# Renewing the normalized input ahead of the token-major values in a two-layer encoder trunk

## The chip, the cores and the metric

The kernel runs on one core of a Trainium2 chip. The metric is the time of one execution on the device in microseconds (us). Three runs of the kernel before took 1825.64, 1826.25 and 1828.06 us; the median is 1826.25 us.

The core has several engines that work side by side, each through its own list of instructions in order: TensorE (PE: matrix products into eight PSUM banks; PEld is its weight load), VectorE (DVE: elementwise work), ScalarE (ACT: functions and copies), GpSimd (POOL: here some small elementwise work, and it issues DMAs) and SyncE (SP: it issues the weight loads). They wait for each other by semaphores.

## The reference

Two layers, each with D_MODEL 1024 and 512 tokens:

```python
h = rmsnorm(x, mix_norm[i])
z = h @ w_in[i]
u_rnn, u_gelu, c_q, ckv_rope, fq, fk, fv, f_logit, gate_logit = split_columns(z)
y_a = rglru_branch(u_rnn, u_gelu, ...) @ w_br_a[i]
y_b = mla_branch(c_q, ckv_rope, ...) @ w_br_b[i]
y_c = fox_branch(fq, fk, fv, f_logit, fox_bf[i]) @ w_br_c[i]
g = sigmoid(gate_logit + gate_b[i]).reshape(B, S, 3, D)
merged = g[:, :, 0] * y_a + g[:, :, 1] * y_b + g[:, :, 2] * y_c
x = x + merged @ w_o[i]
# then a SwiGLU feed-forward and a gated per-layer embedding, each added to x
```

`rglru_branch` is a recurrent branch (convolution, gates, a scan over time), `fox_branch` and `mla_branch` are attentions with 8 heads. What matters here is that `h`, the normalized input, is multiplied with many column blocks of `w_in`: the recurrent inputs, the queries, keys and values of the first attention (called fox), the low-rank inputs of the second, and 3 x 8 blocks of merge gates. Normalizing multiplies each channel of x by a gain and each token by one number r, so r can also be applied after a product, to its result.

## The kernel before, in words

**Layout.** Activations lie feature-major: a page has 128 features on the partitions and 512 tokens in the columns. For accuracy every operand is split into a high part (rounded to float32r) and a low remainder, and each product takes three passes: high by high, high by low, low by high (`mm3`, L239). A split costs a copy on ScalarE and a subtraction on VectorE (`split`, L232). A `pr` page holds both parts of 512 columns, and there are 31 of them (L176); a `pf` page holds 512 float32 columns, and there are 20. Both are handed out from lists, first freed, first taken, and so are the 8 PSUM banks.

**Weights.** `Stream` (L85) loads all weights in the order of use, 256 KB at a time, from SyncE's queue, and splits them (L112 on ScalarE, L113 on VectorE) into a ring of eight units of four 128 by 128 tiles. `dense` (L246) multiplies one column block: for each of its weight tiles (8 for the input's products) three products of 512 columns, into one bank, which an eviction function then reads.

**Order.** The program is traced in a `TileContext` with `schedule_with_timeline_sim=True` (L1386): the order of the instructions on each engine is fixed when the kernel is built, from the order of the program and an estimate of when each could start; weight splits get a higher priority (L111). On the chip each engine then keeps this order.

**A layer's mixers** (`mix`, L441). The input comes as eight pages X, which hold x times the gain and not yet times r; r is known later. First come the recurrent branch's inputs, shared keys, the forget gates and the recurrent gates, all with X and with r applied by the evictions (`scaled`, L278). `lru_tail` (L666) is the recurrent branch's elementwise end: for each of four blocks a combination of two operands, a product, a scan (L677), a product and a split into the pages `yA`. Then follow the keys and queries of heads 0 and 1 (`fox_proj(0, X, st["r"])`, L685 to L687), and the token-major values of all heads (`values`, L608 and L688): 96 products of 512 columns with X as the stationary operand, into four banks; the evictions (L628 on ScalarE, L629 on VectorE) apply r with one number per partition.

**Attention** (L751) goes over 8 heads x 4 blocks of 128 queries. For each block it issues the scores, the softmax on VectorE and ScalarE, transposes and, once per head, the product with the values. Between these it takes pieces of other products off a plan, which has a list for each quarter of the 32 blocks: `fp(p, w)` is the key (w=0) or query (w=1) projection of heads 2p and 2p+1 (8 weight tiles), `mg(0, j, yA)` a merge gate from the input (`gate`, L714, 8 tiles) and the recurrent branch's output product (`branch`, L725, 4 tiles). `fill` (L759) takes about the same number of tiles after each block: seven in the first quarter.

**Renewal.** `renorm` (L691) makes normalized pages Xn: it loads a block of x again from memory by a POOL DMA (L695), scales it by gain and r on VectorE (L696, in the trace at the helper's L218), and splits it (in the trace at L233 on ScalarE and L221 on VectorE). Products of Xn need no r afterwards. Before the change the renewal is part of the first quarter's list beside attention, in three pieces: behind `fp(1, 0)`, `mg(0, 0)` and `mg(0, 1)`, which still take X and r. `drop_x` then frees X and r. From `fp(1, 1)` on all products take Xn.

Of the kernel before, what the change touches and what calls it, by code (L numbers as in the profile page):

```python
# [18 lines left out]
KD = D // 128  # L19
# [147 lines left out]
class Trunk:  # L167
# [273 lines left out]
    def mix(self, layer):  # L441
        nc = self.nc
        L, st, X = layer, self.st, self.xp
# [42 lines left out]
        rT = self.cols(NT)  # L486
# [115 lines left out]
        def fox_proj(p, X, r):  # L602
            return [
                self.dense(self.win(L, C_FK + 128 * p), X, ev_heads(kp, p, r, True, False)),
                self.dense(self.win(L, C_FQ + 128 * p), X, ev_heads(qp, p, r, True, True)),
            ]

        def values(spec, X, rT):  # L608

            V = []  # L610
            bs = [self.banks.take() for _ in range(NT)]
            for k, x in enumerate(X):
                wh, wl = self.w.wide(spec + (k,))
                for j in range(NT):
                    c = slice(j * 128, (j + 1) * 128)
                    self.mm3(bs[j][:, :], x.h[:, c], x.l[:, c], wh, wl, k == 0, k == len(X) - 1)
                    yield
            for j in range(NT):
                g = pr.take()
                V.append(g)  # L620
                dst = g.ap.rearrange("p (h t d) -> p h t d", h=HEADS, t=2)
                src = bs[j].rearrange("p (h d) -> p h d", h=HEADS)
                hi = dst[:, :, 0, :]
                if rT is None:
                    self.split(hi, dst[:, :, 1, :], src)
                else:
                    r = rT[:, j:j + 1]
                    self.act(hi, src, AF.Copy, scale=r)  # L628
                    self.stt(dst[:, :, 1, :], src, r, hi.bitcast(F32), ALU.mult, ALU.subtract)  # L629
                self.banks.give(bs[j])  # L630
            self.V = V


        yA = [None] * 4
# [50 lines left out]
        k0, q0 = fox_proj(0, X, st["r"])  # L685
        self.run(k0)
        self.run(q0)  # L687
        self.run(values(("fv", L), X, rT))  # L688
        Xn = [None] * KD

        def renorm(*ks):  # L691

            for k in ks:
                t, p = pf.take(), pr.take()
                nc.gpsimd.dma_start(t.ap, x_dram[k])  # L695
                self.stt(t.ap, t.ap, self.v(L, V_MIX + k), st["r"].ap, ALU.mult, ALU.mult)  # L696
                self.split(p.h, p.l, t.ap)
                t.free()
                Xn[k] = p
            return  # L700
            yield

        def drop_x():
            for p in X:
                p.free()
            st.pop("r").free()
            return
            yield


        merged = [None] * KD
        out_pages = [None] * KD
# [32 lines left out]
        def merge(n, j, ys, X=Xn, r=None):  # L745
            box = []
            yield from gate(n, j, box, X, r)
            yield from branch(n, j, ys, box)
# [154 lines left out]
        def fp(p, w, X=Xn, r=None):  # L903
            return (fox_proj(p, X, r)[w], 8)

        def mg(n, j, ys, X=Xn, r=None):
            return (merge(n, j, ys, X, r), 12)
# [56 lines left out]
        def done_c():  # L964
            for p in oC:
# [5 lines left out]
        lkv = [(latent(ckv, skv, C_CKV, j), 8) for j in range(2)]  # L971
        tail = chain(gate(2, 2, boxes[2, 2]), gate(2, 3, boxes[2, 3]))
        attention(True, oC, [
            [fp(1, 0, X, st["r"]), (renorm(0, 1), 0), mg(0, 0, yA, X, st["r"]), (renorm(2, 3, 4), 0),
             mg(0, 1, yA, X, st["r"]), (renorm(5, 6, 7), 0), (drop_x(), 0), fp(1, 1), mg(0, 2, yA)],
            [fp(2, 0), mg(0, 3, yA), mg(0, 4, yA), fp(2, 1), mg(0, 5, yA)],
            [fp(3, 0), mg(0, 6, yA), fp(3, 1)] + lq,
            lkv + [mg(0, 7, yA), (free_yA(), 0), (latent_sums(), 0), gt(2, 0), (latent_norm(), 0),
# [413 lines left out]
```

## Time and profile before

| | |
|---|---|
| median of three runs | 1826.25 us (1825.64 to 1828.06) |
| the profiled execution: its own time | 1826.21 us |
| its span, first to last instruction | 1824.4 us |
| mean granted TensorE clock | 0.994 |
| layer 0: values products begin, end | 82.2 us, 104.0 us |
| layer 1: values products begin, end | 975.8 us, 997.6 us |
| weight splits over the span | 590 in the ring and 16 kept, 0.62 us on ScalarE and 0.69 us on VectorE each |

How to read the lines that are shown below: a line of the timeline has the start and the length in us, the engine, the line of the kernel (often a helper's: L237 is `mm`, L218 a combination of a tensor, a number and a tensor, L221 a plain two-operand operation, L225 a scaling, L230 a ScalarE function, L233 the copy of a split), the operation, the tile written and the tiles read, and the shapes; in brackets the idle time ahead of it with what ended it. A group has the same names, then the count, the busy time in us and the mean length in ns, then the idle time before. A line of the waits has who waited for whom, the sum in us, the count and the longest. Matmuls are pipelined, and a matmul's length holds the pipeline's depth: the pace is the distance from start to start. Names: `pf` and `pr` are the pages, `bank` PSUM, `hl` the split weights, `raw` the loaded ones, `vec` the gains, `small` numbers per token.

### The profile page before, as it was taken

The numbers are of one execution on the slowest core, as the hardware profiler recorded it, in microseconds if no ns is written. First come the engines' busy times: TensorE is split into PE (matmuls) and PEld (weight loads), VectorE is DVE, ScalarE is ACT, GpSimd is POOL, SyncE is SP. The second block draws the span as 40 slices with busy tenths as digits, with TensorE's granted clock in tenths as the row PEclk, the third lists the DMA queues.
The fourth block names the chain that finished last, engine by engine and source line by source line (L and its number), as shares of the span: only waits on it lengthen the run. The fifth ranks groups of instructions, "written<-read, shape, count | busy, mean of one in ns | idle before, by whom it ended". The sixth has DMA issues, their size and how long they took to land. (4 is left out here: it accounts for less than half of the span.)

```text
span 1824.4 us, 24163 instructions
## 1 busy us (share of the span) xinstructions
PE 1803.9 (99%) x8476; PEld 1504.5 (82%) x8476; DVE 1209.1 (66%) x2421; ACT 817.5 (45%) x1562; POOL 116.8 (6%) x234
## 2 busy tenths in 40 slices
PE   9899999999999999999999999999999999999998
PEld 7688888888888888888888788888888888888887
DVE  8896678866665555444778966888576555553457
ACT  5766556553333333223448655565523333332233
POOL 1230001100000000000103200010000000000000
PEclk9899999999999999999999999999999999999999
DMA  6142224324322233322433322342232323232331
GB/s 206 59 150 83 81 78 116 100 70 139 95 96 95 96 99 98 109 95 98 133 111 123 105 81 82 90 117 85 87 128 92 99 98 97 95 110 99 98 99 47
DMA packets 98826, 184.17 MB, mean 101 GB/s; under 512 B 13552, under 2 KB 14752, under 8 KB 98704
## 3 DMA queue, kind: packets, MB, share of 16 engines
q1 hardware_dynamic: 89280, 162.04, 27.3%
q0 software_dynamic: 8416, 19.45, 3.9%
q8 instruction: 66, 1.08, 0.2%
q10 hardware_dynamic: 1008, 1.14, 0.2%
q14 instruction: 56, 0.46, 0.1%
HBM read 173.98 MB, written 4.21 MB: 98 GB/s over the span
## 5 line engine op out<-in xcount | busy, mean ns | idle before, releaser
L237 PE MATMUL bank<-pr,hl 128*128 128x512 f32 (+1 forms) x6812 | 1602.3, 392 | 7.0 <-ACT pr L233 6.9
L237 PEld LDWEIGHTS bank<-pr,hl 128*128 128x128 f32 (+1 forms) x6812 | 1270.0, 188 | 268.9 <-ACT pr L233 8.6
L112 ACT CAST hl<-raw 128x512 fp32r<-128x512 f32 x590 | 363.8, 618 | 649.4 <-PE bank L237 438.8
L113 DVE TENSOR_TENSOR hl<-raw,hl 128x512 fp32r<-128x512 f32 x590 | 404.4, 686 | 367.9 <-ACT hl L112 352.0
L221 DVE TENSOR_TENSOR pf<-pf 128x512 f32<-128x512 f32 (+3 forms) x235 | 151.2, 651 | 31.9 <-ACT pf L230 29.8
L221 DVE TENSOR_TENSOR pf<-bank,pf 128x512 f32<-128x512 f32 (+3 forms) x198 | 132.9, 676 | 56.9 <-PE bank L237 31.9
L230 ACT ACTIVATE pf<-pf 128x512 f32<-128x512 f32 (+1 forms) x145 | 86.0, 600 | 112.3 <-DVE pf L221 110.0
L237 PE MATMUL bank<-pr 128*128 128x256 f32 (+5 forms) x704 | 119.5, 301 | 3.5 <-ACT pf L230 3.3
L237 PEld LDWEIGHTS bank<-pr 128*128 128x128 f32 (+1 forms) x704 | 103.4, 190 | 13.7 <-ACT pf L230 3.4
L221 DVE TENSOR_TENSOR pr<-pf,pr 128x512 fp32r<-128x512 f32 (+3 forms) x126 | 85.5, 683 | 4.0 <-ACT pr L233 3.1
L230 ACT ACTIVATE pf<-bank,small 128x384 f32<-128x384 f32 (+3 forms) x130 | 68.9, 531 | 42.0 <-DVE small L838 38.6
L233 ACT CAST pr<-pf 128x512 fp32r<-128x512 f32 (+2 forms) x114 | 70.3, 620 | 29.2 <-DVE pf L218 18.1
L855 ACT CAST pth<-bank 128x128 fp32r<-128x128 f32 (+3 forms) x128 | 54.0, 426 | 65.4 <-PE bank L830 62.3
L838 DVE TENSOR_REDUCE small<-bank 128x1 f32<-128x384 f32 (+3 forms) x128 | 61.7, 484 | 19.2 <-PE bank L237 18.2
L221 DVE TENSOR_TENSOR ptl<-bank,pth 128x128 fp32r<-128x128 f32 (+3 forms) x128 | 61.7, 484 | 12.8 <-ACT pth L855 10.3
L237 PE MATMUL bank<-hl,pr 128*128 128x512 f32 x240 | 55.9, 390 | 0.0
L830 PE MATMUL bank<-identr,pf 128*128 128x128 f32 x320 | 55.7, 273 | 0.0
L237 PEld LDWEIGHTS bank<-hl,pr 128*128 128x128 f32 x240 | 44.9, 188 | 9.2
L225 DVE TENSOR_SCALAR pf<-pf,small 128x384 f32<-128x384 f32 (+3 forms) x128 | 48.4, 383 | 2.6
L230 ACT ACTIVATE pf<-bank,vec 128x512 f32<-128x512 f32 x60 | 41.0, 688 | 16.7 <-PE bank L237 16.2
L218 DVE SCALAR_TENSOR_TENSOR pf<-pf,bank 128x512 f32<-128x512 f32 x48 | 32.6, 683 | 20.8 <-PE bank L237 20.5
L830 PEld LDWEIGHTS bank<-identr,pf 128*128 128x128 f32 x320 | 40.0, 141 | 7.6
(112 smaller groups left out, 792.9 us busy)
## 6 DMA issues: line engine op xcount, KB each, us to landing
raw<-wst SPq DMA_DIRECT2D x606, 256.0 KB, 2.6
pf<-xT POOLq DMA_DIRECT2D x16, 256.0 KB, 3.1
pr<-pr POOLq DMA_DIRECT2D x32, 128.0 KB, 2.7
pf<-xs POOLq DMA_DIRECT2D x16, 256.0 KB, 3.1
pf<-trig POOLq DMA_DIRECT2D x12, 256.0 KB, 3.1
pf<-xT SPq DMA_DIRECT2D x8, 256.0 KB, 5.4
xs<-pf POOLq DMA_DIRECT2D x8, 256.0 KB, 2.7
pf<-pT POOLq DMA_DIRECT2D x4, 256.0 KB, 3.1
```

Of the source, the lines that this page charges most:

```text
L112: self.nc.scalar.copy(hi, src)
L113: self.nc.vector.tensor_tensor(lo, src, hi.bitcast(F32), op=ALU.subtract)
L218: self.nc.vector.scalar_tensor_tensor(out, a, s, b, op0=op0, op1=op1)
L221: self.nc.vector.tensor_tensor(out, a, b, op=op)
L225: self.nc.vector.tensor_scalar(out, a, s1, None, op0=op0)
L230: return self.nc.scalar.activation(out, a, f, **kw)
L233: self.nc.scalar.copy(hi, src)
L237: self.nc.tensor.matmul(out, a, b, start=start, stop=stop, skip_group_check=True)
L830: nc.tensor.transpose(T[:, c], p2.ap[:, c], self.ident[:, :])
L838: nc.vector.reduce_max(R[t][:, 0:1], S[:, :m], axis=AX.X, negate=True)
L855: self.nc.scalar.copy(hi, src)
```

## The change

```diff
         k0, q0 = fox_proj(0, X, st["r"])
         self.run(k0)
         self.run(q0)
-        self.run(values(("fv", L), X, rT))
         Xn = [None] * KD
 
         def renorm(*ks):
...
                 self.split(p.h, p.l, t.ap)
                 t.free()
                 Xn[k] = p
-            return
-            yield
 
         def drop_x():
             for p in X:
                 p.free()
             st.pop("r").free()
-            return
-            yield
-
+
+        renorm(*range(KD))
+        self.run(values(("fv", L), X, rT))
+        drop_x()
...
         attention(True, oC, [
-            [fp(1, 0, X, st["r"]), (renorm(0, 1), 0), mg(0, 0, yA, X, st["r"]), (renorm(2, 3, 4), 0),
-             mg(0, 1, yA, X, st["r"]), (renorm(5, 6, 7), 0), (drop_x(), 0), fp(1, 1), mg(0, 2, yA)],
+            [fp(1, 0), mg(0, 0, yA), mg(0, 1, yA), fp(1, 1), mg(0, 2, yA)],
```

All eight pages are renewed in one call that stands between the keys and queries of heads 0 and 1 and the values, in both layers. The values still take X, and X and r are freed behind them. The key projection of heads 2 and 3 and the first two merge gates take Xn where they took X; their evictions no longer multiply by r, and read the bank directly. Weights, their order and the products are the same.

## The prediction

> **What bounds the kernel now.** I read the page first, then who keeps TensorE waiting, then a table by stage, then the two places of the change row by row, on TensorE and on VectorE.
>
> ```profile
> span 1824.4 us, 24163 instructions
> ...
> PE 1803.9 (99%) x8476; PEld 1504.5 (82%) x8476; DVE 1209.1 (66%) x2421; ACT 817.5 (45%) x1562; POOL 116.8 (6%) x234
> ```
>
> TensorE is busy for 99% of the span; VectorE, with 66%, has room on the average. Who keeps TensorE waiting:
>
> ```profile
> PE bank L237 <- ACT pr L233: 6.9, 3, 3.8
> PE bank L237 <- ACT pf L230: 3.3, 1, 3.3
> ```
>
> The 6.9 us lie in layer 0's start, ahead of anything the change touches. The 3.3 us are a single wait, and it lies in the change's stretch of layer 1. So little can be won, and what can be lost is any time in which a product waits for the renewed input. Whether it will wait is a question to VectorE at that place, not to its average. The table by stage (length, then busy time of PE, PEld, DVE, ACT, POOL, then the granted clock): the first and third rows are the values products of layers 0 and 1, the second a long undisturbed stretch.
>
> ```profile
> 92.00:104.00 12.00, 12.00 (x55) 9.94 (x54) 11.94 (x18) 7.12 (x12) 3.83 (x8) 1.00 0.62 200
> ...
> 300.00:960.00 660.00, 660.00 (x3007) 547.66 (x3006) 407.90 (x743) 250.96 (x462) 24.20 (x45) 1.00 0.32 102
> ...
> 982.00:997.60 15.60, 15.60 (x71) 12.92 (x69) 15.51 (x23) 8.42 (x15) 5.36 (x10) 1.00 0.37 118
> ```
>
> Elsewhere VectorE is busy for 408 of 660 us. Beside the values it is busy for 11.94 of 12.00 us and 15.51 of 15.60 us: it has a queue of its own there, mostly the recurrent branch's tail, which stands ahead of the renewal in the program. This is the row that decides: the change moves a need forward in time, on to an engine that has no free time to serve it sooner.
>
> **The change part by part.** Moved: eight loads, eight scalings (L696), eight copies on ScalarE and eight subtractions on VectorE (both from `split`), per layer. Before, the first projection beside attention and two gates read the raw X, so renewed pages were wanted only 32 weight tiles behind the values. After it, the first product that follows the values wants page 0, and one more page with each three products. TensorE at that place in layer 0, and then in layer 1:
>
> ```profile
> 103.97 0.33 PE L237 MATMUL bank<-pr 128*128 128x128 f32 x2
> 104.14 5.03 PE L237 MATMUL bank<-pr,hl 128*128 128x512 f32 x21
> 109.00 0.40 PE L237 MATMUL bank<-pr 128*128 128x256 f32 x2
> 109.23 4.95 PE L237 MATMUL bank<-pr,hl 128*128 128x512 f32 x21
> ```
>
> ```profile
> 997.66 2.96 PE L237 MATMUL bank<-pr,hl 128*128 128x512 f32 x12
> ...
> 1002.90 1.32 PE L237 MATMUL bank<-pr,hl 128*128 128x512 f32 x5
> ```
>
> From 104.14 to 109.00 us are 21 products: 0.231 us each, 0.69 us for the three of a page. The projection `fp(1, 0)` has 24; its last three run from 109.23 and end at 109.9 us. In layer 1 they run from 1002.90 and end at 1003.6 us.
>
> When are the pages ready? VectorE in layer 0 (four scalings, with a subtraction, a weight split and the first eviction of the values among them):
>
> ```profile
> 103.50 0.74 DVE L218 SCALAR_TENSOR_TENSOR pf<-pf,vec 128x512 f32<-128x512 f32 x1
> 104.17 0.68 DVE L221 TENSOR_TENSOR pr<-pf,pr 128x512 fp32r<-128x512 f32 x1
> 104.77 0.74 DVE L218 SCALAR_TENSOR_TENSOR pf<-pf,vec 128x512 f32<-128x512 f32 x1
> 105.44 0.68 DVE L113 TENSOR_TENSOR hl<-raw,hl 128x512 fp32r<-128x512 f32 x1
> 106.04 0.68 DVE L221 TENSOR_TENSOR pr<-pf,pr 128x512 fp32r<-128x512 f32 x1
> ...
> 109.17 0.74 DVE L218 SCALAR_TENSOR_TENSOR pf<-pf,vec 128x512 f32<-128x512 f32 x1
> 109.83 0.74 DVE L218 SCALAR_TENSOR_TENSOR pr<-bank,small,pr 128x512 fp32r<-128x512 f32 x1
> ```
>
> From start to start a scaling takes 0.67 us and a subtraction or a weight split 0.60 us, so a page costs 1.27 us against the 0.69 us in which TensorE uses it up. What VectorE has from 103.4 us on (layer 0), and from 1003.6 us on (layer 1):
>
> ```profile
> L221 DVE TENSOR_TENSOR pr<-pf,pr 128x512 fp32r<-128x512 f32 x11 | 7.4, 677 | 0.0
> ...
> L218 DVE SCALAR_TENSOR_TENSOR pf<-pf,vec 128x512 f32<-128x512 f32 x8 | 5.9, 739 | 0.0
> L218 DVE SCALAR_TENSOR_TENSOR pr<-bank,small,pr 128x512 fp32r<-128x512 f32 x4 | 2.9, 737 | 0.0
> ...
> L218 DVE SCALAR_TENSOR_TENSOR pf<-pf 128x512 f32<-128x512 f32 x1 | 0.7, 678 | 0.0
> ```
>
> ```profile
> L221 DVE TENSOR_TENSOR pr<-pf,pr 128x512 fp32r<-128x512 f32 x9 | 6.1, 681 | 0.0
> ...
> L218 DVE SCALAR_TENSOR_TENSOR pf<-pf,vec 128x512 f32<-128x512 f32 x7 | 5.2, 741 | 0.0
> ```
>
> Layer 0: no renewal is done by 103.5 us (all eight scalings are still to come), and all that ran before it stands ahead of it in the program after the change too. To the last page: 8 scalings (5.4) + 11 subtractions, three of them the recurrent branch's (6.6) + that branch's last product (0.6) + two weight splits (1.2) = 13.8 us, so 117.3 us; its three products end 0.7 us later. Against 109.9 us that is **8.1 us late**. Low end: the branch's three subtractions and last product come behind (-2.4), 5.7. High end: the values' four evictions, of a scaling's length, stay ahead (+2.7), 10.8.
>
> Layer 1: 7 scalings (4.7) + 9 subtractions (5.4) + two splits (1.2) = 11.3 us from 1003.6 us: 1014.9, with its products 1015.6. Against 1003.6 us that is **12.0 us late**, from 10.8 (two subtractions behind) to 14.7.
>
> TensorE can fill part of this. The order on each engine is fixed when the kernel is built, from an estimate, and this estimate has VectorE further ahead than the chip has: a values eviction can't have been estimated much before the values' end, yet five scalings stand ahead of the first one in layer 0 (103.50 to 109.83 us above) and three in layer 1. So it sees the remaining 3 or 5 pages fall behind by 1.27 - 0.69 = 0.58 us each, and will pull other products (a gate's, on pages already there) into 1.7 us and 2.9 us. I take these. The ends are 0, the order as written, which the rows of TensorE keep, and 4.9 us, seven tiles pulled ahead. That leaves 6.4 us in layer 0 and 9.1 us in layer 1.
>
> What VectorE's lead costs today goes, since TensorE now waits earlier and VectorE catches up: in layer 1 the 3.3 us, and the slow clock that follows. Rows behind that wait, which ended at about 1021 us:
>
> ```profile
> 1022.00:1024.00 2.00, 2.00 (x7) 1.57 (x6) 2.00 (x4) 0.92 (x4) 2.00 (x5) 0.57 0.09 31
> 1024.00:1026.00 2.00, 2.00 (x7) 1.57 (x6) 2.00 (x5) 0.46 (x2) 0.96 (x2) 0.58 0.58 176
> 1026.00:1028.00 2.00, 2.00 (x11) 1.63 (x10) 2.00 (x8) 1.25 (x2) 0.00 (x0) 1.00 0.29 94
> ```
>
> After 3.3 us without a product the granted clock was 0.57 and 0.58 for four us: (0.43 + 0.42) x 2 = 1.7 us lost. So 3.3 + 1.7 = 5.0 us are given back. The new waits can bring the same: 1.7 us in layer 1, where I expect the first page about 4 us after the values, between the 2.5 us that I take for layer 0 and the 6 us after which the other seven scalings start; half of it, 0.8 us, in layer 0, where page 0 should be there at about 106.7 us (the subtraction of 106.04), 2.5 us after the values. The ends are 0 and 3.4 us in each.
>
> The Trainium skill, "TensorE: Matmul & The Clock Gate", Part 1, says that the clock halves after an idle window of about 3.4 us and returns after a busy one. The trace's 3.3 us with two slow rows agree; by that rule layer 0, with waits of under 3.4 us each, would lose nothing and the sum would be 0.8 us lower.
>
> Costed at nothing, with cover. (a) Three VectorE operations go per layer (0.68 us each: the projection's multiplication, two gates' scalings); they come behind the late pages, when VectorE has caught up. Without that cover: -2.0 us a layer. (b) The four evictions of the values, now behind the renewal, hold four of the eight banks longer; the other four are free for the first two score products, the projection and the first gate. Without that: up to 2.7 us, the high ends above. (c) The eight loads move up on POOL's queue, past the copies of forget rows (L589) of the first heads. Those and the first loads:
>
> ```profile
> 89.44 3.15 POOL L589 DMA_DIRECT2D pr<-pr  x6 [9.70 <-DVE pr L221]
> 92.58 0.58 POOL L695 DMA_DIRECT2D pf<-xT  x1
> ```
>
> The copies are wanted by the scores of 103.97 us, 11 us after they are issued, so a load ahead of them that waits for its page hides; without the cover it costs that wait. (d) Pages: 8 raw, 8 renewed, 4 values, 4 of heads 0 and 1, 4 recurrent and 1 shared make 29 of 31, so nothing waits for one.
>
> Sum: 6.4 + 0.8 + 9.1 + 1.7 - 5.0 = **+13.0 us**. The profiled execution took 1826.2 us (its span and 1.8 us around it), the median of the runs 1826.25 us; so 1826.2 + 13.0 = **1839 us**. With every low end it is 5.7 - 4.9 + 10.8 - 4.9 - 5.0 = +1.7 us, with every high end 10.8 + 3.4 + 14.7 + 3.4 - 5.0 = +27.3 us; both extremes at once in both layers are not likely, and I take 1828 to 1852 us as this case's own range.
>
> **The rivals.** *No change (about 1826 us).* TensorE is as busy as before with the same products, and the order fixed at build time fills the wait: projection, gate and second gate run page by page, 2.1 us of work for each 1.27 us page. Then only page 0 is waited for, 2.5 us and about 4 us, against the 5.0 us given back: +1.5 us. For it: all that this needs is in the program. Against it: the estimate sees pages earlier than the chip has them, so it has no cause to pull that much. The Trainium skill, "Perfetto Trace Analysis", Identifying the Most-Contended Engine, would have the most occupied engine improved first, and by that too a shift on VectorE gives no change; the full rows beside the values speak against it.
>
> *Faster (1821 us).* The renewal passes the recurrent tail on VectorE, as loads can now be issued earlier; all pages are there in time, and the 3.3 + 1.7 us of layer 1 go: -5.0 us. It decides at page 7: it must be subtracted by 104.14 + 7 x 0.69 = 109.0 us. Then 4.8 us of the 13.8 us of work may not lie ahead of it in layer 0, and less than half of it in layer 1. Against it: the tail stands first in the program and its inputs are there.
>
> *No effect on order.* VectorE already renews as soon as it is free of the tail; the edit may leave its order as it was. TensorE waits all the same, with the evictions in between: this is the high end, +27 us at most.
>
> **How the numbers follow.** A measurement here can tell 0.2%, 3.7 us, from no change. The forecast has 0.76, its low edge lying 1.9 us under that bound for little of its chance; no change 0.14; faster 0.10. The range reaches from 1824 us, taking in most of the no-change case, to 1853 us, past the likeliest one's end for the high ends. Chances: faster 0.10, same 0.14, slower 0.76.
>
> **What would show it.** Right: after the values, waits of TensorE for VectorE's `pr` of L221 in both layers, some 6 and 9 us with the products between them; the wait of 3.3 us for ScalarE's `pf` gone; a granted clock near 0.5 behind the values of layer 1; scalings in front of the values' evictions on VectorE. Wrong: products of a gate between those of the projection, page by page, with under 3 us of waits; or VectorE's scalings ahead of the recurrent scans.

## The result and the profile after

The changed kernel takes **1847.88 us** (median of four runs, 1846.92 to 1848.43), against 1827.13 us for the kernel before in the same runs: a ratio of 1.0114, with a 95% interval of 1.0096 to 1.0131, so 21 us slower. The forecast was slower, 1839 us, with a range of 1824 to 1853 us.

The page of the profiled execution (1848.43 us): the work is the same, the span is 22.3 us longer, and TensorE is busy for a smaller share.

```profile
span 1846.7 us, 24159 instructions
...
PE 1810.9 (98%) x8476; PEld 1506.9 (82%) x8476; DVE 1210.4 (66%) x2415; ACT 815.9 (44%) x1562; POOL 116.1 (6%) x234
```

Who keeps TensorE waiting (sum, count, longest). Most of the second row is still the start of layer 0; the single wait of 3.3 us for ScalarE's `pf` has gone, and the rest is new.

```profile
PE bank L237 <- DVE pr L218: 10.2, 4, 5.2
PE bank L237 <- ACT pr L233: 7.5, 5, 3.8
PE bank L237 <- POOL pr L587: 4.2, 1, 4.2
PE bank L237 <- ACT pf L230: 1.6, 2, 0.8
PE bank L237 <- DVE pr L221: 1.6, 2, 0.9
```

Where they lie: TensorE's timeline of layer 0, from the values (the first row) on.

```profile
81.83 21.92 PE L237 MATMUL bank<-hl,pr 128*128 128x512 f32 x96
103.59 0.33 PE L237 MATMUL bank<-pr 128*128 128x128 f32 x2
103.76 0.92 PE L237 MATMUL bank<-pr,hl 128*128 128x512 f32 x3
104.51 0.41 PE L237 MATMUL bank<-pr 128*128 128x256 f32 x2
104.75 0.84 PE L237 MATMUL bank<-pr,hl 128*128 128x512 f32 x3
110.85 1.01 PE L237 MATMUL bank<-pr 128*128 128x384 f32 x2 [5.25 <-DVE pr L218]
112.83 5.20 PE L237 MATMUL bank<-pr,hl 128*128 128x512 f32 x15 [0.97 <-DVE pr L218]
118.26 0.98 PE L237 MATMUL bank<-pr,hl 128*128 128x512 f32 x3 [0.24 <-ACT pr L233]
120.03 0.74 PE L237 MATMUL bank<-pr 128*128 128x512 f32 x2 [0.79 <-ACT pf L230]
121.41 8.01 PE L237 MATMUL bank<-pr,hl 128*128 128x512 f32 x34 [0.64 <-DVE pr L221]
```

Where before the 24 products of one projection ran with only two short score products between them, there are now three of the projection, three of a gate, and then a stop: the third score product (384 columns) stands next and waits 5.25 us. The waits add up to 7.9 us. The same in layer 1:

```profile
985.90 21.92 PE L237 MATMUL bank<-hl,pr 128*128 128x512 f32 x96
...
1009.09 0.50 PE L237 MATMUL bank<-pr 128*128 128x128 f32 x2 [0.59 <-ACT pr L566]
1014.49 0.77 PE L237 MATMUL bank<-pr 68*128 68x128 f32 x2 [4.20 <-POOL pr L587]
1018.95 1.01 PE L237 MATMUL bank<-pr 128*128 128x384 f32 x2 [3.70 <-DVE pr L218]
1020.27 5.44 PE L237 MATMUL bank<-pr,hl 128*128 128x512 f32 x15 [0.31 <-DVE pr L218]
1026.62 0.96 PE L237 MATMUL bank<-pr,hl 128*128 128x512 f32 x3 [0.92 <-ACT pr L233]
1028.39 0.73 PE L237 MATMUL bank<-pr 128*128 128x512 f32 x2 [0.81 <-ACT pf L230]
1030.04 9.63 PE L237 MATMUL bank<-pr,hl 128*128 128x512 f32 x34 [0.92 <-DVE pr L221]
```

These are 11.5 us. The two starts of the values tell the layers apart: they stood at 82.2 and 975.8 us, and stand at 81.8 and 985.9, so layer 0 lost 10.4 us and all that follows 985.9 us another 12.2 us. The clock tells the rest (the columns as in the prediction; the granted clock is the third number from the end):

```profile
109.00:116.00 7.00, 4.18 (x10) 3.00 (x11) 7.00 (x13) 2.65 (x5) 0.00 (x0) 0.52 0.22 64
...
1014.00:1024.00 10.00, 5.51 (x13) 3.96 (x14) 9.94 (x18) 3.29 (x7) 2.06 (x4) 0.50 0.42 133
...
1031.00:1034.00 3.00, 3.00 (x9) 2.33 (x8) 1.93 (x5) 1.23 (x3) 0.00 (x0) 0.50 0.01 1
```

TensorE worked for 4.18 us at about half clock in layer 0, and for 5.51 + 3.0 us in layer 1: half of that is lost, 2.0 and 4.3 us. Waits and clock together: 7.9 + 2.0 + 11.5 + 4.3 = 25.7 us, less the 5.0 us that went (3.3 us of wait, 1.7 us of clock), 20.7 us of the 22.2 us between the two profiled executions.

VectorE in layer 0 shows why (the first page's scaling; a scaling and two evictions of the values; the last subtraction of a page):

```profile
85.61 0.75 DVE L218 SCALAR_TENSOR_TENSOR pf<-pf,vec 128x512 f32<-128x512 f32 x1
...
109.38 0.75 DVE L218 SCALAR_TENSOR_TENSOR pf<-pf,vec 128x512 f32<-128x512 f32 x1
110.04 1.41 DVE L218 SCALAR_TENSOR_TENSOR pr<-bank,small,pr 128x512 fp32r<-128x512 f32 x2
...
121.98 0.70 DVE L221 TENSOR_TENSOR pr<-pf,pr 128x512 fp32r<-128x512 f32 x1
```

One page was scaled early, at 85.6 us, ahead of most of the recurrent tail, so that the first products wait for nothing. The last was there at 122.7 us. The values' first two evictions start at 110.04 us, and as the first ends, at about 110.8 us, the score product that waits for its bank starts: the wait's name, VectorE's `pr` of L218, is the eviction.

So three theories were to be told apart. **P**: VectorE's queue delivers late what the first products need, the renewed pages above all. **B**: the bank is the cause; had the score product not been pulled ahead on to a bank of the values, TensorE would have gone on. **Q**: the loads, moved ahead on POOL's queue, delay the first heads' rows (the 4.20 us named after POOL in layer 1).

### The profile page after: what moved, and what is told of

It reads as the page before. It is cut to its first block, busy times and chain, and to the rows that moved or that the text cites. A ratio compares the mean times of both kernels' runs of the same rounds, so it can differ in the third digit from the quotient of the medians.

```text
span 1846.7 us, 24159 instructions
## 1 busy us (share of the span) xinstructions
PE 1810.9 (98%) x8476; PEld 1506.9 (82%) x8476; DVE 1210.4 (66%) x2415; ACT 815.9 (44%) x1562; POOL 116.1 (6%) x234
## 5 line engine op out<-in xcount | busy, mean ns | idle before, releaser
L237 PE MATMUL bank<-pr,hl 128*128 128x512 f32 (+1 forms) x6812 | 1607.4, 393 | 10.4 <-ACT pr L233 7.5
L237 PEld LDWEIGHTS bank<-pr,hl 128*128 128x128 f32 (+1 forms) x6812 | 1271.4, 189 | 275.2 <-ACT pr L233 10.4
L221 DVE TENSOR_TENSOR pf<-pf 128x512 f32<-128x512 f32 (+3 forms) x235 | 151.7, 654 | 32.1 <-ACT pf L230 30.0
L221 DVE TENSOR_TENSOR pf<-bank,pf 128x512 f32<-128x512 f32 (+3 forms) x192 | 128.9, 677 | 58.0 <-PE bank L237 31.8
L237 PE MATMUL bank<-pr 128*128 128x256 f32 (+4 forms) x704 | 121.2, 303 | 15.3 <-DVE pr L218 8.9
L230 ACT ACTIVATE pf<-bank,small 128x512 f32<-128x512 f32 (+3 forms) x130 | 68.9, 531 | 38.6 <-DVE small L836 35.5
L221 DVE TENSOR_TENSOR pr<-pf,pr 128x512 fp32r<-128x512 f32 (+3 forms) x122 | 82.8, 685 | 4.7 <-ACT pr L233 3.9
L836 DVE TENSOR_REDUCE small<-bank 128x1 f32<-128x128 f32 (+3 forms) x128 | 62.1, 487 | 19.4 <-PE bank L237 18.2
L221 DVE TENSOR_TENSOR ptl<-bank,pth 128x128 fp32r<-128x128 f32 (+3 forms) x128 | 62.2, 486 | 13.9 <-ACT pth L853 11.9
L225 DVE TENSOR_SCALAR pf<-pf,small 128x128 f32<-128x128 f32 (+3 forms) x128 | 48.7, 384 | 3.0
L218 DVE SCALAR_TENSOR_TENSOR pf<-pf,bank 128x512 f32<-128x512 f32 x48 | 32.9, 688 | 22.0 <-PE bank L237 21.4
```

The lines of the kernel that those rows point to most:

```text
L218: self.nc.vector.scalar_tensor_tensor(out, a, s, b, op0=op0, op1=op1)
L221: self.nc.vector.tensor_tensor(out, a, b, op=op)
L225: self.nc.vector.tensor_scalar(out, a, s1, None, op0=op0)
L230: return self.nc.scalar.activation(out, a, f, **kw)
L237: self.nc.tensor.matmul(out, a, b, start=start, stop=stop, skip_group_check=True)
L836: nc.vector.reduce_max(R[t][:, 0:1], S[:, :m], axis=AX.X, negate=True)
```

## The experiments

**Move without need.** The renewal ahead of the values, as in the change; the first products as before.

```diff
         self.run(values(("fv", L), X, rT))
-        drop_x()
...
-            [fp(1, 0), mg(0, 0, yA), mg(0, 1, yA), fp(1, 1), mg(0, 2, yA)],
+            [fp(1, 0, X, st["r"]), mg(0, 0, yA, X, st["r"]), mg(0, 1, yA, X, st["r"]), (drop_later(), 0),
+             fp(1, 1), mg(0, 2, yA)],
```

> The renewal stays where the change puts it, ahead of the values, but the first projection and the first two gates take X and r again, as before; X and r are freed behind them. Theory P (the pages: TensorE loses the time because its first products want pages that VectorE has not finished) expects the loss to go: 1826 to 1830 us, the upper end for values evictions that come 2.7 us later on VectorE. Theory B (the banks: TensorE stands at a score product that was pulled ahead and wants a bank whose values eviction now lies behind the renewal) expects the same here, since that score product stands 40 products further on. Theory Q (the queue of POOL: loads moved ahead delay the rows that the first heads' scores need) expects 3 to 5 us of the loss to stay: 1829 to 1832 us.

1826.61 us, a ratio of 1.0001 (0.9992 to 1.0011): all of the loss is gone. The order on TensorE is that of before up to the second gate. The stage that follows the values, in layer 0 and in layer 1:

```profile
103.50:125.00 21.50, 20.84 (x94) 17.09 (x94) 21.50 (x39) 14.35 (x25) 7.79 (x17) 1.00 0.36 112
...
996.40:1020.00 23.60, 21.31 (x93) 16.48 (x91) 23.54 (x40) 15.18 (x27) 6.49 (x13) 1.00 0.40 124
```

VectorE is busy for 21.50 of 21.50 us, and TensorE works for 20.84 of them. In layer 1 TensorE still stands for 2.3 of 23.6 us, without a slow clock, where the kernel before had its 3.3 us and 1.7 us of slow clock. So VectorE's full queue costs no more here than in the kernel before, nor does the renewal's place in it: the early need is what costs. Q falls with this as a cause of more than 2 us, since the loads stand where the change puts them.

**Need without move.** The renewal behind the values, at the head of the first list; all products take the renewed input.

```diff
-            [fp(1, 0, X, st["r"]), (renorm(0, 1), 0), mg(0, 0, yA, X, st["r"]), (renorm(2, 3, 4), 0),
-             mg(0, 1, yA, X, st["r"]), (renorm(5, 6, 7), 0), (drop_x(), 0), fp(1, 1), mg(0, 2, yA)],
+            [(renorm(*range(KD)), 0), (drop_x(), 0), fp(1, 0), mg(0, 0, yA), mg(0, 1, yA), fp(1, 1), mg(0, 2, yA)],
```

> The renewal goes behind the values, to the head of the first list beside attention, and all products beside attention take the renewed input. P expects the loss to stay or grow, since the pages come no earlier: 1844 to 1856 us. B expects most of the two longest waits (5.2 and 3.7 us) to go, because the evictions of the values now stand ahead of the renewal on VectorE: 1836 to 1841 us. Q expects the 4 us of layer 1 to go: 1842 to 1845 us.

1855.96 us, 1.0162 (1.0147 to 1.0177): the early need, with the renewal behind the values, costs 30 us, and moving the renewal ahead, the other half of the change, gives 8 us of them back. The range of P held, B's and Q's didn't. The pages come in another order here, page 0 as the seventh, so a part of the 30 us may be that order's.

**Evictions with a priority.**

```diff
+                    with self.tc.high_priority():
                         self.act(hi, src, AF.Copy, scale=r)
                         self.stt(dst[:, :, 1, :], src, r, hi.bitcast(F32), ALU.mult, ALU.subtract)
```

> The changed kernel, with the evictions of the values set ahead of the renewal by a priority; the order on TensorE is the same. B expects the waits for VectorE's L218 (10.2 us in both layers) to go for the most part: 1838 to 1842 us. P expects the wait to move to the next product that wants a page, with the last page at the same time or later: 1846 to 1850 us. Q expects 1848 us.

1847.69 us, 1.0118 (1.0103 to 1.0133). This doesn't tell P from B: the priority left the evictions nearly where they were (in layer 0 VectorE's start from 110.48 to 114.78 us, in the changed kernel from 110.04 to 114.94 us), as the wait shows.

```profile
111.29 1.01 PE L237 MATMUL bank<-pr 128*128 128x384 f32 x2 [5.43 <-DVE pr L218]
```

**Loads by SyncE.**

```diff
-                nc.gpsimd.dma_start(t.ap, x_dram[k])
+                nc.sync.dma_start(t.ap, x_dram[k])
```

> The changed kernel, with the eight loads of the renewal issued by SyncE, beside the weights, and not by POOL. Q expects layer 1 to get back 3 to 5 us: 1843 to 1845 us. P and B expect no change beyond 1.5 us: 1846 to 1850 us.

1846.24 us, 1.0109 (1.0094 to 1.0124), whose interval is about that of the changed kernel. The waits change their names and hardly their sum: the POOL row is gone, and these stand in its place.

```profile
PE bank L237 <- DVE pr L218: 14.9, 4, 8.0
...
PE bank L237 <- issue: 4.8, 1, 4.8
```

**Renewal ahead of the recurrent tail.** The same work in another order.

```diff
+        renorm(*range(KD))
         lru_tail()
         k0, q0 = fox_proj(0, X, st["r"])
...
-        renorm(*range(KD))
         self.run(values(("fv", L), X, rT))
```

> The changed kernel with the renewal ahead of the recurrent branch's tail and of the keys and queries of heads 0 and 1, so that VectorE does it first; the work is the same. Theory P (the order on VectorE puts the pages too late for the first products) expects most of the 21 us back: 1826 to 1833 us, with the recurrent tail and the scores late in place of the pages, where TensorE has projection and two gates to do. A rival, theory V (VectorE simply has more work here than fits beside the products, so that any order costs the same), expects 1843 to 1850 us.

1841.53 us, 1.0084 (1.0069 to 1.0099): 6 us back, short of what P expected and more than V did. The intended order came about only in part: in layer 0 scalings stand at 84.4, 86.9, 97.3 us, and the last at 120.3 us. The tail holds 16 of the 20 `pf` pages that the loads also need. So the pages stay late, and TensorE waits for them directly:

```profile
107.44 0.50 PE L237 MATMUL bank<-pr,hl 128*128 128x512 f32 x1 [1.53 <-ACT pr L233]
111.34 15.69 PE L237 MATMUL bank<-pr,hl 128*128 128x512 f32 x58 [3.40 <-DVE pr L221]
```

**Subtractions on GpSimd.**

```diff
-                self.split(p.h, p.l, t.ap)
+                nc.scalar.copy(p.h, t.ap)
+                nc.gpsimd.tensor_tensor(p.l, t.ap, p.h.bitcast(F32), op=ALU.subtract)
```

> The changed kernel with the renewal's eight subtractions per layer on GpSimd in place of VectorE, which takes 8 x 0.6 = 4.8 us per layer off VectorE's queue. P and V expect 4 to 10 us back: 1838 to 1844 us. If GpSimd takes over 1.3 us for one, it becomes the late one itself, and the time stays at 1846 us or more.

1858.53 us, 1.0177 (1.0162 to 1.0192), 11 us slower than the change. The condition set down for this was met, GpSimd takes 1.42 us for one:

```profile
L697 POOL TENSOR_TENSOR pr<-pf,pr 128x512 fp32r<-128x512 f32 x8 | 11.3, 1418 | 8.2 <-ACT pr L696 7.0 <-PE bank L237 1.1
```

**The other way: renewal later.** The kernel before, with the renewal behind the second gate, and all products of the first list with X.

```diff
-            [fp(1, 0, X, st["r"]), (renorm(0, 1), 0), mg(0, 0, yA, X, st["r"]), (renorm(2, 3, 4), 0),
-             mg(0, 1, yA, X, st["r"]), (renorm(5, 6, 7), 0), (drop_x(), 0), fp(1, 1), mg(0, 2, yA)],
+            [fp(1, 0, X, st["r"]), mg(0, 0, yA, X, st["r"]), mg(0, 1, yA, X, st["r"]), (renorm(0, 1, 2), 0),
+             fp(1, 1, X, st["r"]), (renorm(3, 4, 5), 0), mg(0, 2, yA, X, st["r"]), (renorm(6, 7), 0), (drop_x(), 0)],
```

> The other way: the kernel before, with the renewal later, spread behind the second gate, the second projection and the third gate beside attention; all products of the first list take X and r. That takes the renewal's 10 us of VectorE per layer out of the stretch where it is full, and adds two operations that apply r. P expects TensorE's wait in layer 1 (3.3 us and 1.7 us of slow clock) to go: 1820 to 1823 us. V's counterpart, a VectorE that stays full because the other work moves up, expects 1825 to 1828 us.

1822.96 us, 0.9981 (0.9971 to 0.9990): faster than both kernels, than the one before by 0.2%, as P expected. Layer 1 behind the values:

```profile
997.00:1022.00 25.00, 23.93 (x109) 19.55 (x108) 24.84 (x45) 19.23 (x36) 2.15 (x4) 1.00 0.45 137
1022.00:1033.00 11.00, 10.04 (x51) 8.21 (x50) 10.58 (x29) 7.74 (x18) 6.81 (x13) 1.00 0.54 169
```

VectorE is as full as ever (V was right in that), but TensorE stands for only 1.1 and 1.0 us, and the clock stays at 1.00 where the kernel before had 0.84 in the same eleven us.

**Banks emptied by ScalarE.**

```diff
-                    r = rT[:, j:j + 1]
-                    self.act(hi, src, AF.Copy, scale=r)
-                    self.stt(dst[:, :, 1, :], src, r, hi.bitcast(F32), ALU.mult, ALU.subtract)
+                    t = pf.take()
+                    self.act(t.ap, bs[j][:, :], AF.Copy, scale=rT[:, j:j + 1])
+                    src = t.ap.rearrange("p (h d) -> p h d", h=HEADS)
+                    self.split(hi, dst[:, :, 1, :], src)
+                    t.free()
```

> The changed kernel with the values' banks emptied by ScalarE alone (a scaled copy to a page, split from there), so that no bank waits for VectorE; VectorE has the same number of operations, ScalarE four copies of 0.69 us more per layer; the order of the first products on TensorE is the same. Theory B (the score product that stands before a values bank) expects the waits of 5.2 and 3.7 us for VectorE's L218 to go and 7 to 10 us with them: 1838 to 1841 us. P expects the same time to be waited at the next products, for the recurrent pages and the renewed ones: 1845 to 1849 us.

1850.85 us, 1.0134 (1.0117 to 1.0151). Now the third score product finds its bank at once, and the time moves on to the next needs:

```profile
105.61 0.50 PE L237 MATMUL bank<-pr 128*128 128x384 f32 x2
...
111.62 0.49 PE L237 MATMUL bank<-pr,hl 128*128 128x512 f32 x1 [1.68 <-ACT pr L233]
116.59 2.50 PE L237 MATMUL bank<-pr,hl 128*128 128x512 f32 x5 [4.47 <-ACT pr L233]
...
121.80 8.48 PE L237 MATMUL bank<-pr,hl 128*128 128x512 f32 x24 [1.86 <-DVE pr L221]
```

The long run of products starts at 121.80 us, in the changed kernel at 121.41 us. B falls as the cause: the bank was only the first of several needs in the same queue.

**A shorter and a longer queue.** Two kernels; the first sets the low parts of the renewed pages to zero, on ScalarE.

```diff
-                self.split(p.h, p.l, t.ap)
+                nc.scalar.copy(p.h, t.ap)
+                self.act(p.l, t.ap, AF.Copy, scale=0.0)
```

> The changed kernel without the renewal's eight subtractions per layer: the low parts of the renewed pages are set to zero by ScalarE, so the products' low terms of these pages are left out, while every product is still done. VectorE's queue up to the last page is 8 x 0.6 = 4.8 us shorter per layer. Theory P (the pages and what else the first products need come off VectorE's queue too late) expects 8 to 13 us back, the 9.6 us and some of the slow clock: 1835 to 1840 us. If the loss hung on something else than the length of that queue, the time would stay within 2 us of 1848.

```diff
                 self.split(p.h, p.l, t.ap)
+                self.tt(p.l, t.ap, p.h.bitcast(F32), ALU.subtract)
```

> The changed kernel with each of the renewal's subtractions done twice on VectorE (the second writes the same values again): 4.8 us more per layer in the queue. P expects 8 to 14 us more: 1856 to 1862 us. If VectorE had room there, the time would stay at 1848 us.

The longer queue gives 1861.53 us, 1.0191 (1.0176 to 1.0206): 13.7 us more for 9.6 us of VectorE, as expected. The shorter one gives 1842.87 us, 1.0090 (1.0075 to 1.0106): 5.0 us back for 9.6, half of what P expected. Its layer 0:

```profile
109.42 0.73 PE L237 MATMUL bank<-pr 128*128 128x384 f32 x2 [4.18 <-DVE pr L218]
113.11 13.73 PE L237 MATMUL bank<-pr,hl 128*128 128x512 f32 x52 [2.97 <-DVE pr L218]
```

With the pages early, the values' evictions are what TensorE waits for until 113.1 us: what this edit takes off the pages, the bank holds.

**Both at once.** The banks emptied by ScalarE and the low parts at zero; the edit is the two diffs above together.

> The changed kernel with both edits at once: the values' banks emptied by ScalarE alone (e8_banks_by_scalar), and the renewal without its subtractions, the low parts set to zero (e9_no_low), so that the products' low terms of these pages are left out. Each edit alone moved the time little: +3.0 us and -5.0 us. If the pages and the values' evictions are two needs in one queue, each of which covers for the other, both together give far more than the sum: 1829 to 1836 us. If the two edits simply add, 1844 to 1848 us. ScalarE has 12 operations more per layer than in the changed kernel, which could keep the time above 1836 us.

1844.06 us, 1.0100 (1.0083 to 1.0117). Neither bank nor low parts are in the way, and 18 us of loss remain; the theory that these two only cover for each other falls. Layer 0 now waits for ScalarE's copy out of the bank, then for the recurrent branch's last page, then for a renewed page:

```profile
108.19 3.23 PE L237 MATMUL bank<-pr,hl 128*128 128x512 f32 x13 [2.04 <-ACT pf L230]
114.15 1.22 PE L237 MATMUL bank<-pr,hl 128*128 128x512 f32 x2 [2.73 <-DVE pr L221]
116.61 10.40 PE L237 MATMUL bank<-pr,hl 128*128 128x512 f32 x37 [1.24 <-ACT pr L698]
```

**A smaller need.** The changed kernel, but the first projection takes X.

```diff
-        drop_x()
...
-            [fp(1, 0), mg(0, 0, yA), mg(0, 1, yA), fp(1, 1), mg(0, 2, yA)],
+            [fp(1, 0, X, st["r"]), (drop_later(), 0), mg(0, 0, yA), mg(0, 1, yA), fp(1, 1), mg(0, 2, yA)],
```

> The changed kernel, but the first projection beside attention takes X and r again; the gates take the renewed input. The first need for a page thus moves back by 24 products, 5.5 us. P expects the loss to fall by about that per layer and the slow clock with it: 1831 to 1838 us. If one early need were as costly as any, it stays at 1845 us or more; if only the first product mattered, it goes to 1826 us.

1841.11 us, 1.0076 (1.0059 to 1.0093): 6.8 us back for 24 products (5.5 us) of cover per layer, less than the 10 to 17 us expected and far from all. With the two gates on X as well, 72 products in all, everything is back (the first experiment). TensorE needs the whole of that cover.

## Why the prediction was right, and where its sizes were off

The mechanism was the one forecast: TensorE's first products behind the values want pages that VectorE, full at that place, delivers too late; the 3.3 us of layer 1 and its slow clock are given back. The experiment that undoes the need alone shows it, and so does the one that only lengthens the queue. Its signs came only in part. The 3.3 us wait is gone, the clock behind the values of layer 1 is at 0.50, and four scalings stand in front of the first eviction of the values in layer 0. But of the waits behind the values only 0.64 and 0.92 us are named after L221; the longest are named after the evictions (L218), and that the same time is waited for the pages once a bank is free was shown only by an experiment. The rivals of no change and of a gain didn't come: products of the gates and of the recurrent branch do stand between those of the projection, but 7.9 and 11.5 us of waits remain, and the renewal didn't pass the recurrent tail, one page apart.

The sum was +13.0 us, the measurement +20.8 us. Term by term:

- **The last page.** 117.3 us forecast in layer 0, 122.7 us measured. This is the high end and more: the four evictions stayed ahead (2.7 us), and so did the recurrent tail's last scan, which starts at 103.33 us, two more weight splits, and masks and maxima of score products. The step that failed is the choice between the ends: that evictions, which the change puts behind the renewal in the program, come behind it on VectorE. The prediction itself had shown the estimate to be ahead of the chip at this place, which speaks for the high end.
- **The order of the pages.** The prediction let the pages come in the order in which a product takes them, and under (d) it counted `pr` pages, but not the 20 `pf` pages into which the loads go. In the instruction list as built, which has the numbers of the buffers, the loads of the changed kernel come for pages 0, 2, 3, 6, 7, 4, 1 and 5 in both layers: pages 1 and 5 were given `pf` pages that the recurrent tail holds until its first two blocks are split. GpSimd's timeline of layer 0 has these two late, while the other six are issued by 97.5 us:

```profile
103.72 0.56 POOL L694 DMA_DIRECT2D pf<-xT  x1 [4.30 <-DVE pr L221]
...
106.03 0.56 POOL L694 DMA_DIRECT2D pf<-xT  x1 [0.78 <-DVE pr L221]
```

VectorE scales page 1 as the seventh, at 116.80 us, though every product takes it second, and TensorE's last wait in layer 0, which ends at 121.41 us, is for this page and not for page 7. So are the last waits there in three of the experiments above: 1.86 us with the banks emptied by ScalarE, 4.17 us with the longer queue, 1.24 us with both at once.
- **The fill.** 1.7 and 2.9 us were taken; up to the wait that ends at 121.41 us the order as built puts 20 products of the gates and the recurrent branch ahead of the rest of the projection in layer 0, 4.6 us, near the end of 4.9 us, and behind that wait 12 more of the first gate ahead of the projection's last eight. Behind the first score product of layer 0 the list goes on like this (bank, product, count; bank 68 is the projection's, 70 and 72 the gates', 67 the recurrent branch's, 69 and 71 those of score products):

```
MATMUL bank_68<-pr,hl 128x512 x3
MATMUL bank_69<-pr 128x256 x2
MATMUL bank_70<-pr,hl 128x512 x3
MATMUL bank_71<-pr 128x384 x2
MATMUL bank_67<-pr,hl 128x512 x10
MATMUL bank_72<-pr,hl 128x512 x3
MATMUL bank_67<-pr,hl 128x512 x2
```

- **The waits.** The later page and the greater fill nearly cancel: 6.4 us forecast for layer 0 and 7.9 measured, 9.1 and 11.5 in layer 1.
- **The cover of (b), the banks.** "The other four are free for the first two score products, the projection and the first gate" was so, but the third score product, bank 71, was itself pulled ahead, and it stands in front of all else for 5.25 and 3.70 us. The cover was gone; yet the experiment with the free bank shows that this cost nothing by itself, as the next needs were as late.
- **The clock.** 0.8 and 1.7 us forecast, 2.0 and 4.3 measured. In layer 0 the wait was taken as 2.5 us and a trickle; it was one of 5.25 us, and the clock stood at 0.52 for seven us. By the rule of the Trainium skill that the prediction named ("TensorE: Matmul & The Clock Gate", Part 1) a wait of that length does halve the clock, so rule and trace agree here too; it was the length of the wait that was off. In layer 1 the slow stretch lasted ten us, as TensorE went on to stop and go in it.
- **The cover of (c), POOL's queue.** In layer 1 TensorE waits 4.20 us for the second part of the first score product; at 1014.49 us, when it starts, VectorE has just finished the first of the subtractions of 64 rows for these heads (a row of its timeline starts at 1013.71 us). I read that wait as one more item of VectorE's queue: in the instruction list as built this product waits for that subtraction, and with the loads on SyncE it starts, at 1014.80 us, again as such a subtraction ends (1014.02 us and 0.68 us long). Moving the loads off POOL's queue changed the time by -1.6 us, within the intervals. Whether POOL's order had a share below that stays open.
- **Page 0** was expected at 106.7 us and was there before the values ended. That changed no sum, since page 1 was not.

What stays open is how the loss divides among the needs: with the bank, the pages' low parts or the first projection's need taken away one at a time, between -3 and 7 us come back, and with the first two together still only 4 us. The loss isn't a sum of parts, since each need hides the next; of what was tried only a cover of independent products removed it. A rival to that reading is untested: page 1 comes seventh in all the experiments that took one need away, and no run gave the pages in the order of need and left the rest alone. (With the renewal ahead of the tail they come as 0, 2, 1, 3, 5, 4, 6, 7, but there the loads lack `pf` pages.) What that order alone would give back stays open.

## What to carry to other kernels

An operand that is renewed "in time" must be judged by the queue of the engine that makes it, at that place, not by that engine's average: here VectorE was 66% busy over the span and full beside and behind the values (39.5 of 40.0 us from 85 us on, in the kernel before). Products that can run on the older form of an operand are cover; taking them away exposes everything that is late in that queue at once, and then no single repair that was tried here gave the time back. Where a queue is full, put needed-late work later still: moving the renewal behind the products that don't need it gave the only version faster than both. And where buffers are handed out in order of release, look at which loads get those that come free last: here one was that of the second page.

## What the runs showed of the hardware that was not expected

- A subtraction of 128x512 elements takes 1.42 us on GpSimd here, against 0.69 us on VectorE, so GpSimd, 6% busy in the changed kernel, was no relief for 16 of them.
- Single waits of about 1 us left the granted clock at 1.00 in the later renewal, while each wait of over 3 us, before and after, was followed by 3 to 10 us at about 0.5. So was the end of layer 1's stretch in the changed kernel, where three waits of 0.8 to 0.9 us had five products between them: 0.50 from 1031 to 1034 us. The 5.25 us wait thus cost some 2 us more than its length, an estimate from the 4.18 us of work at half clock.
- The same 9.6 us of VectorE work were worth 13.7 us when added and 5.0 us when taken away (with as many operations more on ScalarE): a queue that several needs share answers unevenly.
